# A gated DeltaNet layer: one decay matrix per unit in place of two

## The chip, the cores and the metric

One core of one Trainium2 chip runs the whole program in one launch. The metric is device time in microseconds. Three timed runs gave 2041.48, 2045.49 and 2047.63 us, so the median is 2045.49 us.

## What is computed

A trunk of two layers over 1024 tokens of width 1024, all in float32. The first layer is a gated DeltaNet, the second a softmax attention with a forget gate; the change lies in the first alone. Its core, for one value head and one chunk of tokens, with `g` the running sum of the log decay inside the chunk:

```python
decay = exp(where(lower, g[:, None] - g[None, :], -inf))
L = where(strict, (k * beta) @ k.T * decay, 0.0)
T = triangular_solve(eye + L, eye)
u = T @ (v * beta);  w = T @ (k * beta * exp(g))
attn = (q @ k.T) * decay
v_new = u - w @ state
o = (q * exp(g)) @ state + attn @ v_new
state = state * exp(g[-1]) + (k * exp(g[-1] - g)).T @ v_new
```

`k` and `q` are normalised to length one per token. There are 8 key heads and 16 value heads, so two value heads share the keys and queries of one key head. The output is normalised per head, multiplied with a gate `silu(z)` and projected back to width 1024.

## The kernel before

The tokens are taken in two halves of 512, each half in four chunks of 128 (the kernel's chunk; the result doesn't depend on it). A **unit** is one key head with its two value heads for one half: 8 groups x 2 halves = 16 units. For each unit the projections write keys, queries and values with the channels on the partitions, and then these stages run:

- `prepk`: `decay(t, "d1")` makes the matrix `d1[p, f] = exp(g_p - g_f)` for p > f, zero elsewhere, for 2 heads x 4 chunks (8 blocks of 128x128). It loads the row of `g` to all partitions (`gb`, 512 KB), masks it on GpSimd (`affine_select`) and takes eight exponentials on ScalarE. Then the keys are transposed (`to_tokens`), the strengths `un`, `wn` and `weg` are made from `beta` and the key norms `rk`, and `L` is written over `d1` as `wn * (k k^T) * d1`.
- `invert_blocks`: the 16x16 blocks on the diagonal of I + L are inverted by substitution on VectorE (`xi`, `xtmp`), with DMAs through DRAM (`lb`, `lr`, `rb`) that bring them to a suitable layout and back into `r` (`rmat`).
- `invert_merge`: three doubling steps of small matmuls (16, 32 and 64 wide) fill `r`, which holds the inverse transposed. VectorE makes the transposed diagonal blocks `tm` (`tmat`) with `nc.vector.transpose` on lines 1095 and 1125 and a scaling on line 1150. In each step the first matmuls read `lm` and `r`, the second ones read `tm`.
- `prepv`: the queries and values are transposed; the values are scaled by `un` on GpSimd (line 921).
- `prep2`: `decay(t, "d2")` makes `d2[s, t] = exp(g_t - g_s)` for t >= s, with a second load of `gb`, a second mask and eight more exponentials; then `exp(gb)` scales the queries (`qd`) and `d2` becomes the attention matrix `am`.
- `chain`: four chunks one after the other. `ch` matmuls give `k^T state` and then `T` times the corrected values, both in PSUM tile `p1`; `vn` (ScalarE copy, line 973) and `ve` (VectorE, line 974) are taken from `p1`; the `co` matmuls use them for the output and the new state.
- `finish`: the output of a unit is normalised, transposed, gated (`ogt`), split into a high and a low part (`ogh`, `ogl`) and stored.

TensorE's instruction order is written out by a planner, `Flow`, at build time: every stage is a generator that yields estimated waits (constants named `Y_...`, in ns), and whoever is due goes next. The projections have the last priority and fill what is left. The other engines' order comes from a scheduler with a model of time. Every engine then runs its own list in order, and every DMA is issued by SyncE in order. `at(shape, name, bufs)` takes a tile from a ring of `bufs` buffers: `gb` has 1, `d1` and `d2` have 2 each.

A matrix is split into a high and a low part for the projections (`mm3`: three matmuls for each pair).

Of the kernel before, what the change touches and what calls it, by code (L numbers as in the profile page):

```python
# [8 lines left out]
F32 = mybir.dt.float32  # L9
F32R = mybir.dt.float32r  # L10
# [5 lines left out]
P = 128  # L16
D = 1024
# [20 lines left out]
Y_PK = 1200  # L38
# [4 lines left out]
Y_P2 = 4000  # L43
# [10 lines left out]
Y_F1 = 800  # L54
Y_F2 = 2550
# [127 lines left out]
def tile_trunk(  # L183
# [308 lines left out]
    with ExitStack() as sa:  # L492
# [34 lines left out]
        def start_norm():  # L527
            xsT = [at([P, HALF], n, b) for n, b in (("k", KQ), ("k", KQ), ("k", KQ), ("q", 2), ("q", 2))]
            xsT += [at([P, HALF], "ktok", 3) for _ in range(3)]
            for t in range(CPH):  # L530
                xt = at([P, D], *(("vtok", 3), ("qd", 2))[t // 2])
                nc.sync.dma_start(xt, x[t * P : (t + 1) * P, :])
                for d in norm_tile(xt, at([P, D], "ogt", 1), lambda k, p, t=t: nc.scalar.copy(
                    xsT[k][:, t * P : (t + 1) * P], p)):
                    flow.t += d
            tags = [("d1", 2), ("og", 2), ("zg", ZG), ("d1", 2), ("og", 2), ("zg", ZG), ("gb", 1)]
# [10 lines left out]
            for n in range(2):  # L547
                ps = banks[n]
                acc = at([P, D], "d2", 2)
# [43 lines left out]
        def norm_tile(xt, jk, evac):  # L593
            rs = rms_rows(xt, jk, at)
# [13 lines left out]
        def next_norm():  # L608
            yield from hold(lambda: done["kqv"] >= 2)
            for t in range(CPH):  # L610
# [6 lines left out]
                hf = at([P, KT, P], "nh", 1)  # L617

                def evac(k, p):
                    nc.vector.tensor_scalar(  # L620
                        hf[:, k], p, gcol[0][:, k : k + 1], scol[0][:, k : k + 1],
                        op0=ALU.mult, op1=ALU.add,
                    )

                yield from norm_tile(xt, hf.rearrange("p k t -> p (k t)"), evac)
                yield 3000
                nc.sync.dma_start(
                    h1_d[:, :, t * P : (t + 1) * P].rearrange("k p t -> p k t"), hf
                )
# [12 lines left out]
        def gates(h, gt):  # L642
# [44 lines left out]
            nc.scalar.activation(ex, ex, AF.Exp)  # L687
            ngc = at([P, CPH, 16], "g_ngc", 2)
# [12 lines left out]
            gt.update(col=col, ex=ex, ngc=ngc, beta=beta, g_d=g_d)  # L701
# [132 lines left out]
        def decay(t, name):  # L834
            gb = at([P, 2, HALF], "gb", 1)
# [5 lines left out]
            dv = at([P, 2 * CPH, P], name, 2)  # L841
            low = name == "d1"
            nc.gpsimd.affine_select(
                out=dv, in_=gb.rearrange("p j (c t) -> p (j c) t", t=P),
                compare_op=ALU.is_gt if low else ALU.is_ge, fill=BIG if low else -BIG, base=0,
                pattern=[[0, 2 * CPH], [-1 if low else 1, P]], channel_multiplier=1 if low else -1,
            )
            bias = t["gt"]["col" if low else "ngc"]
            yield Y_DG
            for j in range(2):  # L850
                for c in range(CPH):
# [4 lines left out]
                        dv[:, u], dv[:, u], AF.Exp, scale=-1.0 if low else 1.0, bias=bias[:, c, hd : hd + 1]  # L856
                    )
            return gb, dv

        def prepk(t):  # L860
            g, gt, kf = t["g"], t["gt"], t["k"]
            _, d1v = yield from decay(t, "d1")
            yield Y_PK
            t["ktok"] = ktok = at([P, CPH, P], "ktok", 3)
            t["ss"] = ss = at([P, 2, CPH], "gss", 3)
# [3 lines left out]
            nc.vector.tensor_scalar(rk, ss[:, 0], EPS, None, op0=ALU.add)  # L869
            nc.gpsimd.tensor_tensor(rk, rk, mhalf[:, 0:CPH], op=ALU.pow)  # L870
            rkb = bc(rk, 2, 2)
            t["un"] = un = at([P, CPH, 2], "un", 3)
            t["wn"] = wn = at([P, CPH, 2], "wn", 2)
            t["weg"] = weg = at([P, CPH, 2], "weg", 3)
            nc.vector.tensor_tensor(un, gt["beta"][:, :, 2 * g : 2 * g + 2], rkb, op=ALU.mult)
            nc.vector.tensor_tensor(wn, un, rkb, op=ALU.mult)
            nc.vector.scalar_tensor_tensor(
                weg, wn, -1.0, gt["ex"][:, 1, :, 2 * g : 2 * g + 2], op0=ALU.mult, op1=ALU.mult
            )
            t["lm"] = d1v  # L880
# [27 lines left out]
        def prepv(t):  # L908
# [4 lines left out]
            for j in range(2):  # L913
                yield Y_PT
                yield from to_tokens(vt[:, j], vtok[:, :, j], None)
# [4 lines left out]
            for c in range(CPH):  # L920
                nc.gpsimd.tensor_tensor(vtok[:, c], vtok[:, c], bc(t["un"][:, c], 2, P), op=ALU.mult)
            yield 0

        def prep2(t):
            kf, qf = t["k"], t["q"]
            gb, d2 = yield from decay(t, "d2")
            t["am"] = am = d2.rearrange("p (j c) t -> p j c t", c=CPH)
            t["qd"] = qd = at([P, 2, CPH, P], "qd", 2)
            for j in range(2):
                yield 2 * Y_DX  # L930
                nc.scalar.activation(gb[:, j], gb[:, j], AF.Exp)
# [12 lines left out]
        def chain(t):  # L944
            h, g, gt, kf, r = t["h"], t["g"], t["gt"], t["k"], t["r"]
            ktok, qd, am, uv, weg, epo, ex = t["ktok"], t["qd"], t["am"], t["uv"], t["weg"], t["epo"], gt["ex"]
# [3 lines left out]
            for c in range(CPH):  # L950
# [4 lines left out]
                else:  # L955
                    mm(p1[:, 0:256], kf[:, c], st)
                    xt = at([P, 2 * P], "xp", 2)
                    for j in range(2):
                        sl = slice(j * P, (j + 1) * P)
                        nc.vector.scalar_tensor_tensor(  # L960
                            xt[:, sl], p1[:, sl], weg[:, c, j : j + 1], uv[:, c, j],
# [4 lines left out]
                for j in range(2):  # L966
# [6 lines left out]
                nc.scalar.copy(vn, p1[:, 256:512])  # L973
                nc.vector.tensor_tensor(
                    ve, p1[:, 256:512].rearrange("p (j f) -> p j f", f=P),
                    bc(ex[:, 0, c, 2 * g : 2 * g + 2], 2, P), op=ALU.mult,
# [36 lines left out]
        def finish(t, og, so):  # L1013
# [10 lines left out]
            ogt = at([P, 2, HALF], "ogt", 1)  # L1024
            for j in range(2):
                tr = yield from pst("tr", 2)
                for c in range(CPH):
                    tr_(tr[:, c * P : (c + 1) * P], og[:, c, j], ident)
                nc.vector.scalar_tensor_tensor(
                    ogt[:, j], tr, nw_h, zg[:, j], op0=ALU.mult, op1=ALU.mult  # L1030
                )
                flow.free(tr, R_T)
                yield Y_F1 if j == 0 else Y_F2
            ogh = at([P, 2, HALF], "ogh", 1, F32R)
            ogl = at([P, 2, HALF], "ogl", 1, F32R)
            for j in range(2):
                split(ogh[:, j], ogl[:, j], ogt[:, j], lo_eng=nc.vector)
                yield 1500
# [783 lines left out]
```

## Time and profile before

| | |
|---|---|
| median of three runs | 2045.49 us |
| the profiled execution's own time | 2046.11 us |
| its span, first to last instruction | 2044.3 us |
| TensorE busy (matmul) | 1852.2 us, 91% |
| VectorE busy | 1378.0 us, 67% |
| ScalarE busy | 1036.5 us, 51% |
| GpSimd busy | 484.5 us, 24% |
| mean granted TensorE clock | 0.954 of 2.4 GHz |

The profile is of one execution. "Busy" is the time in which at least one instruction of an engine runs; matmul ends are modelled. A wait names the instruction whose semaphore came last. PE is the matmul part of TensorE, PEld its weight loads, DVE VectorE, ACT ScalarE, POOL GpSimd and SP SyncE, which issues the DMAs. `d` stands for both decay matrices in the rows, `g_gc` marks the exponentials of the first and `g_ngc` those of the second. The units of the DeltaNet layer run from about 85 us to about 1100 us of the span; the output projection of that layer and the second layer follow.

### The profile page before, as it was taken

The numbers are of one execution on the slowest core, as the hardware profiler recorded it, in microseconds if no ns is written. First come the engines' busy times: TensorE is split into PE (matmuls) and PEld (weight loads), VectorE is DVE, ScalarE is ACT, GpSimd is POOL, SyncE is SP. The second block draws the span as 40 slices with busy tenths as digits, with TensorE's granted clock in tenths as the row PEclk, the third lists the DMA queues.
The fourth block names the chain that finished last, engine by engine and source line by source line (L and its number), as shares of the span: only waits on it lengthen the run. The fifth ranks groups of instructions, "written<-read, shape, count | busy, mean of one in ns | idle before, by whom it ended". The sixth has DMA issues, their size and how long they took to land.

```text
span 2044.3 us, 36353 instructions
## 1 busy us (share of the span) xinstructions
PE 1852.2 (91%) x12940; PEld 1546.6 (76%) x12940; DVE 1378.0 (67%) x3319; ACT 1036.5 (51%) x2684; POOL 484.5 (24%) x518
## 2 busy tenths in 40 slices
PE   4888898898998989999989788999999999999898
PEld 4666677777776777777877677889889889889676
DVE  5788888787868566766656576446656666666664
ACT  3554566555545445555444444246655655655631
POOL 2050232121213021222101322421231331331222
PEclk7988899999999999999999989999999999999899
DMA  6677676666555445454469988210210220111523
GB/s 246 222 244 236 199 254 198 217 228 219 184 175 158 153 142 175 155 154 131 143 216 316 306 307 279 80 53 32 63 60 19 60 65 21 58 62 38 170 84 96
DMA packets 236870, 317.83 MB, mean 155 GB/s; under 512 B 103752, under 2 KB 156512, under 8 KB 236688
## 3 DMA queue, kind: packets, MB, share of 16 engines
q1 hardware_dynamic: 236688, 315.51, 47.6%
q8 instruction: 102, 1.67, 0.3%
q14 instruction: 80, 0.66, 0.1%
HBM read 233.76 MB, written 81.67 MB: 154 GB/s over the span
## 4 chain that ended last, share of the span: by engine, by line
PE 54%; DVE 16%; DMA 16%; ACT 5%; issue 4%; SPq 3%; POOL 2%; DVEq 0%; POOLq 0%; ACTq 0%
PE mm L128 35%; PE lg L128 5%; PE pt L132 3%; PE oT L128 3%; DVE wlo L327 2%; PE tr L132 2%; PE co L128 2%; PE su L128 2%; DMA lr<-lb 2%; DMA wraw<-in_wb_dram 2%; DMA oraw<-in_ada_w_dram 2%; DVE cv_y L746 2%; DVE xtmp L1068 1%; DVE d L887 1%; DVE xi L1072 1%
## 5 line engine op out<-in xcount | busy, mean ns | idle before, releaser
L128 PE MATMUL mm<-ht_h,whi 128*128 128x512 f32 x784 | 352.8, 450 | 11.0 <-DVE olo L300 8.0
L128 PE MATMUL mm<-ht_l,whi 128*128 128x512 f32 x784 | 318.2, 406 | 3.9 <-DVE ht_l L583 3.9
L128 PE MATMUL mm<-ht_h,wlo 128*128 128x512 f32 x784 | 318.3, 406 | 1.7 <-POOL wlo L327 1.7
L128 PE MATMUL mm<-whi,h_h 128*128 128x384 f32 x512 | 186.9, 365 | 1.4 <-ACT whi L324 1.4
L128 PEld LDWEIGHTS mm<-ht_h,whi 128*128 128x128 f32 x784 | 154.9, 198 | 43.7 <-DVE olo L300 9.0
L128 PEld LDWEIGHTS mm<-ht_h,wlo 128*128 128x128 f32 x784 | 153.9, 196 | 37.7 <-POOL wlo L327 2.2
L128 PEld LDWEIGHTS mm<-ht_l,whi 128*128 128x128 f32 x784 | 155.2, 198 | 30.8 <-DVE ht_l L583 5.2
L128 PE MATMUL mm<-wlo,h_h 128*128 128x384 f32 x512 | 174.1, 340 | 2.7 <-POOL wlo L327 2.7
L746 DVE SCALAR_TENSOR_TENSOR cv_y<-cv_t,conv_h,cv_y 128x512 f32<-128x512 f32 x192 | 146.1, 761 | 42.3 <-ACT cv_y L738 40.1
L128 PE MATMUL mm<-whi,h_l 128*128 128x384 f32 x512 | 173.4, 339 | 0.0
L1562 DVE TENSOR_TENSOR ptl<-pt,pth 128x512 fp32r<-128x512 f32 x192 | 106.3, 555 | 85.2 <-ACT pth L1561 83.4
L1561 ACT CAST pth<-pt 128x512 fp32r<-128x512 f32 x192 | 91.2, 476 | 131.1 <-PE pt L132 130.1
L1405 POOL TENSOR_TENSOR rs<-ss,mhalf 128x4 f32<-128x4 f32 x64 | 64.5, 1007 | 314.4 <-DVE ss L1403 309.0
L327 DVE TENSOR_TENSOR wlo<-ht_h,whi 128x512 fp32r<-128x512 f32 x124 | 94.1, 802 | 52.9 <-ACT whi L324 46.5
L1526 ACT ACTIVATE lg<-lg,mx 128x896 f32<-128x896 f32 (+7 forms) x128 | 99.5, 778 | 54.5 <-DVE mx L1518 50.3
L324 ACT CAST whi<-ht_h 128x512 fp32r<-128x512 f32 x124 | 70.6, 619 | 103.7 <-DMA ht_h<-in_wa_o_dram 34.1
L128 PEld LDWEIGHTS mm<-wlo,h_h 128*128 128x128 f32 x512 | 97.7, 191 | 6.4 <-POOL wlo L327 4.4
L128 PEld LDWEIGHTS mm<-whi,h_h 128*128 128x128 f32 x512 | 98.2, 192 | 4.0 <-ACT whi L324 1.7
L128 PE MATMUL mm<-h_h,whi 128*128 128x512 f32 x240 | 100.5, 419 | 0.6 <-DVE wlo L1661 0.3
L324 ACT CAST whi<-wlo 128x512 fp32r<-128x512 f32 (+1 forms) x108 | 62.6, 626 | 72.8 <-PE mm L128 34.4
L132 PE MATMUL pt<-ident,lg 128*128 128x128 f32 (+1 forms) x584 | 96.0, 274 | 3.0 <-ACT lg L1526 3.0
L128 PEld LDWEIGHTS mm<-whi,h_l 128*128 128x128 f32 x512 | 97.1, 190 | 0.0
(355 smaller groups left out, 4715.6 us busy)
## 6 DMA issues: line engine op xcount, KB each, us to landing
ht_h<-in_wa_o_dram SPq DMA_DIRECT2D x62, 512.0 KB
wc<-whi SPq DMA_DIRECT2D x45, 512.0 KB
wc<-wlo SPq DMA_DIRECT2D x45, 512.0 KB
wlo<-wc SPq DMA_DIRECT2D x45, 512.0 KB
whi<-wc SPq DMA_DIRECT2D x45, 512.0 KB
wlo<-in_wa_c_dram SPq DMA_DIRECT2D x35, 512.0 KB
oraw<-in_ada_w_dram SPq DMA_DIRECT2D x128, 128.0 KB
gb<-g_d SPq DMA_DIRECT2D x32, 512.0 KB
```

What stands on the lines that cost most here:

```text
L128: self.nc.tensor.matmul(out, lhsT, rhs, start=start, stop=stop)
L132: self.nc.tensor.transpose(out, src, ident)
L324: nc.scalar.copy(hi, src)
L327: (lo_eng or nc.gpsimd).tensor_tensor(lo, src, hi.bitcast(F32), op=ALU.subtract)
L746: nc.vector.scalar_tensor_tensor(y, raw[:, j : j + HALF], w[:, j : j + 1], y, op0=ALU.mult, op1=ALU.add)
L887: nc.vector.scalar_tensor_tensor(d1v[:, u], mq[:, c * P : (c + 1) * P], wn[:, c, j : j + 1], d1v[:, u], op0=ALU.mult, op1=ALU.mult,)
L1068: nc.vector.tensor_tensor(tv, bc(lr[:, j + 1 :, j], 1, m), xi[:, 0:m, j : j + 1].broadcast_to([P, m, n]), op=ALU.mult,)
L1072: nc.vector.tensor_tensor(xi[:, 0:m, j + 1 :], xi[:, 0:m, j + 1 :], tv, op=ALU.subtract)
L1405: nc.gpsimd.tensor_tensor(rs, ss, mhalf[:, 0:4], op=ALU.pow)
L1526: nc.scalar.activation(lg, lg, AF.Exp, scale=-1.0, bias=mx[:, hh : hh + 1], accum_out=sums[:, tt : tt + 1],)
L1561: nc.scalar.copy(ph_[:, cs], pp[:, cs])
L1562: nc.vector.tensor_tensor(pl_[:, cs], pp[:, cs], ph_[:, cs].bitcast(F32), op=ALU.subtract)
```

## The change

- One decay matrix per unit. `decay` makes only `d2` (mask, eight exponentials) and takes `exp(gb)` right behind. `prepk` calls it ahead of the transposes of the keys; `prep2` makes none.
- `lm` is now a tile of its own (ring `d1`), written as `wn * (k k^T) * d2`, so it is the transpose of what it was, with the strength `wn` on the other side (a similarity by a diagonal). The inverse then acts on values that carry no strength: `xp` is `uv - exp(g) * (k^T state)` (`neg`), the values are divided by the key norm where they are taken from PSUM (ScalarE with `scale=irk`, four operations of 128x256 in place of two copies of 128x512 and four products on GpSimd), and `wn` is applied behind the inverse: `vn` is two scaled ScalarE operations of 128x128 in place of one copy of 128x256, and `ve` is scaled by `wex`.
- In `invert_merge` the roles swap: the first matmuls of each step read `lm` and `tm`, the second ones read `r`.
- Rings: `gb` 2 (was 1), `d2` 3 (was 2). The tiles `ogt`, `ogh`, `ogl` and `nh` hold half of what they did, one buffer each: `finish` now does one head at a time (transpose, gate, split, store with two DMAs of 256 KB), and the normalisation of the second half of the tokens stores in two pieces.
- Planner constants: `Y_PK` 1200 to 1000, `Y_P2` 4000 to 3000, `Y_F1` 800 to 900, `Y_F2` 2550 to 1600.

```diff
 def decay(t):
-    gb = at([P, 2, HALF], "gb", 1)
+    gb = at([P, 2, HALF], "gb", 2)
...
-    dv = at([P, 2 * CPH, P], name, 2)
+    dv = at([P, 2 * CPH, P], "d2", 3)
...
+    for j in range(2):
+        yield 2 * Y_DX
+        nc.scalar.activation(gb[:, j], gb[:, j], AF.Exp)
     return gb, dv
 def prepk(t):
-    _, d1v = yield from decay(t, "d1")
-    yield Y_PK
+    t["gb"], t["d2"] = yield from decay(t)
     yield from to_tokens(kf, ktok, ss[:, 0])
...
+    t["lm"] = lm = at([P, 2 * CPH, P], "d1", 2)
     nc.vector.scalar_tensor_tensor(
-        d1v[:, u], mq[:, c * P : (c + 1) * P], wn[:, c, j : j + 1], d1v[:, u],
+        lm[:, u], mq[:, c * P : (c + 1) * P], wn[:, c, j : j + 1], t["d2"][:, u],
 def prepv(t):
+    nc.scalar.activation(
+        vtok[:, c].rearrange("p j f -> p (j f)"), tr[:, o : o + 2 * P], AF.Copy,
+        scale=t["irk"][:, c : c + 1],
+    )
...
-    for c in range(CPH):
-        nc.gpsimd.tensor_tensor(vtok[:, c], vtok[:, c], bc(t["un"][:, c], 2, P), op=ALU.mult)
 def chain(t):
-    nc.scalar.copy(vn, p1[:, 256:512])
+    for j in range(2):
+        nc.scalar.activation(
+            vn[:, j * P : (j + 1) * P], p1[:, 256 + j * P : 256 + (j + 1) * P], AF.Copy,
+            scale=wn[:, c, j : j + 1],
+        )
 def finish(t, og, so):
-    ogt = at([P, 2, HALF], "ogt", 1)
     for j in range(2):
...
+        ogt = at([P, HALF], "ogt", 1)
...
+        ogh, ogl = at([P, HALF], "ogh", 1, F32R), at([P, HALF], "ogl", 1, F32R)
+        split(ogh, ogl, ogt, lo_eng=nc.vector)
 def invert_merge(t):
-    mm(pbk[b][o : o + 16, us], lm[sls[b], u, o : o + 16], r[sls[b], u, o + 16 : o + 32])
+    mm(pbk[b][sls[b], us], lm[h16, u, sls[b]], tms[b][0:16, u, 0:16])
...
-    mm(pa_[0:32, us], lm[32:64, u, 0:32], r[32:64, u, 32:64])
+    mm(pa_[32:64, us], lm[0:32, u, 32:64], tm[0:32, u, 0:32])
...
-    mm(p2[0:64, u * 64 : u * 64 + 64], lm[64:128, u, 0:64], r[64:128, u, 64:128])
+    mm(p2[64:128, u * 64 : u * 64 + 64], lm[0:64, u, 64:128], tm[0:64, u])
```

## Rows read from the trace of the kernel before

**Rows 1.** Windows by stage: busy us per engine, granted clock, DMA share, GB/s.

```profile
core 0: us, PE busy (x) PEld busy (x) DVE busy (x) ACT busy (x) POOL busy (x), PEclk, DMA share, GB/s
85.00:1100.00 1015.00, 909.05 (x7907) 738.33 (x7907) 752.46 (x1899) 532.86 (x1592) 218.24 (x274) 0.95 0.61 194
1100.00:1300.00 200.00, 174.30 (x746) 139.99 (x745) 123.03 (x204) 78.53 (x155) 54.97 (x42) 0.92 0.83 282
1300.00:2045.00 745.00, 713.93 (x4061) 622.19 (x4059) 451.07 (x1129) 388.38 (x854) 196.06 (x169) 0.98 0.19 62
```

**Rows 2.** Waits of PE from 85 to 1100 us: total, times, longest.

```profile
PE co L128 <- DVE ve L974: 19.2, 15, 2.4
PE tr L132 <- ACT vtok L905: 16.6, 6, 7.0
PE ch L128 <- DVE xp L960: 12.1, 9, 2.6
PE su L128 <- DMA rmat<-rb: 9.3, 2, 7.7
...
PE co L128 <- ACT vn L973: 7.9, 8, 2.9
PE tr L132 <- ACT ktok L905: 6.4, 1, 6.4
```

**Rows 3.** Groups by line and form, 85 to 1100 us: busy, mean ns, idle before.

```profile
L273 DVE SCALAR_TENSOR_TENSOR ohi<-oraw,cond,ohi 128x256 f32<-128x256 f32 x112 | 64.2, 573 | 14.2 <-DMA oraw<-in_ada_w_dram 13.6
...
L921 POOL TENSOR_TENSOR vtok<-vtok,un 128x256 f32<-128x256 f32 x64 | 44.6, 726 | 81.2 <-ACT vtok L905 81.2
...
L738 ACT ACTIVATE cv_y<-mm,conv_h 128x512 f32<-128x512 f32 x61 | 42.3, 694 | 0.0
...
L855 ACT ACTIVATE d<-d,g_ngc 128x128 f32<-128x128 f32 x128 | 40.9, 390 | 21.8 <-POOL d L843 21.8
L855 ACT ACTIVATE d<-d,g_gc 128x128 f32<-128x128 f32 x128 | 39.1, 390 | 24.1 <-POOL d L843 14.7 <-POOL cv_t L741 9.4
...
L843 POOL TENSOR_SCALAR_AFFINE_SELECT d<-gb 128x1024 f32<-128x1024 f32 x32 | 36.4, 1139 | 117.5 <-PE co L128 52.5 <-DMA gb<-g_d 39.0 <-PE su L128 17.1
...
L737 ACT COPY cv_t<-mm 128x512 f32<-128x512 f32 x60 | 35.1, 584 | 27.6 <-PE mm L128 27.4
...
L973 ACT COPY vn<-ch 128x256 f32<-128x256 f32 x63 | 23.6, 374 | 36.1 <-PE ch L128 35.9
...
L931 ACT ACTIVATE gb<-gb 128x512 f32<-128x512 f32 x32 | 18.4, 617 | 0.0
```

**Rows 4.** Timeline of ACT around the longest wait for `vtok`.

```profile
629.98 0.98 ACT L855 ACTIVATE d<-d,g_ngc 128x128 f32<-128x128 f32 x3 [1.77 <-POOL d L843]
...
632.20 1.26 ACT L855 ACTIVATE d<-d,g_ngc 128x128 f32<-128x128 f32 x4
633.37 0.56 ACT L905 COPY vtok<-tr 128x512 f32<-128x512 f32 x1
```

**Rows 5.** The window right behind that wait.

```profile
632.00:638.80 6.80, 4.82 (x14) 3.94 (x15) 3.42 (x6) 5.25 (x20) 4.11 (x4) 0.50 0.44 107
```

**Rows 6.** One line of VectorE in the whole trace: min/median/max ns.

```profile
L273 DVE SCALAR_TENSOR_TENSOR ohi<-oraw,cond,ohi x112: 430/480/1555, 91.9 to 617.7; 128x256 f32<-128x256 f32 x112
L746 DVE SCALAR_TENSOR_TENSOR cv_y<-cv_t,conv_h,cv_y x192: 697/748/1476, 62.9 to 1011.0; 128x512 f32<-128x512 f32 x192
```

**Rows 7.** Waits of DVE from 85 to 1100 us.

```profile
DVE ve L974 <- ACT vn L973: 10.1, 11, 3.0
```

**Rows 8.** Timeline, first and last of twelve merge steps with late transposes.

```profile
157.60 0.39 PE L128 MATMUL su<-rmat,d 32*16 32x16 f32 x4 [7.66 <-DMA rmat<-rb]
...
160.39 0.44 DVE L1095 STREAM_TRANSPOSE tmat<-rmat 32x256 f32<-32x256 f32 x1
...
1051.98 1.32 DVE L1125 STREAM_TRANSPOSE tmat<-rmat 32x256 f32<-32x256 f32 x3
...
1052.02 0.24 PE L128 MATMUL su<-rmat,d 32*32 32x32 f32 x2 [0.45 <-ACT rmat L1120]
```

**Rows 9.** The chain that ended last: start, us, what; a 512 KB load.

```profile
951.67 6.03 DMA gb<-g_d
```

More of the change, by code (lines that the diff above doesn't have):

```diff
@@ L53 @@
 Y_F0 = 9000
-Y_F1 = 800
-Y_F2 = 2550
+Y_F1 = 900
+Y_F2 = 1600
 Y_R2 = 6400
@@ L593, in norm_tile @@
         def norm_tile(xt, jk, evac):
-            rs = rms_rows(xt, jk, at)
+            if jk is None:
+                ss = at([P, 2], "ln_s2", 2)
+                for c in range(2):
+                    nc.scalar.activation(
+                        at([P, HALF], "nh", 1), xt[:, c * HALF : c * HALF + HALF], AF.Square,
+                        accum_out=ss[:, c : c + 1],
+                    )
+                nc.vector.tensor_tensor(ss[:, 0:1], ss[:, 0:1], ss[:, 1:2], op=ALU.add)
+                nc.vector.tensor_scalar(ss[:, 0:1], ss[:, 0:1], 1.0 / D, EPS, op0=ALU.mult, op1=ALU.add)
+                rs = at([P, 1], "ln_rs", 2)
+                nc.gpsimd.tensor_tensor(rs, ss[:, 0:1], mhalf[:, 0:1], op=ALU.pow)
+            else:
+                rs = rms_rows(xt, jk, at)
             nc.vector.tensor_scalar(xt, xt, rs, None, op0=ALU.mult)
@@ L687, in gates @@
             nc.scalar.activation(ex, ex, AF.Exp)
+            neg = at([P, CPH, 16], "g_neg", 2)
+            nc.vector.tensor_scalar(neg, ex[:, 1], -1.0, None, op0=ALU.mult)
             ngc = at([P, CPH, 16], "g_ngc", 2)
@@ L700, in gates @@
             done["gates"] = h + 1
-            gt.update(col=col, ex=ex, ngc=ngc, beta=beta, g_d=g_d)
+            gt.update(neg=neg, ex=ex, ngc=ngc, beta=beta, g_d=g_d)
         def z_after(i):
@@ L912, in prepv @@
             vtok = at([P, CPH, 2, P], "vtok", 3)
-            for j in range(2):
+            for c0 in range(0, CPH, 2):
                 yield Y_PT
-                yield from to_tokens(vt[:, j], vtok[:, :, j], None)
+                tr = yield from pst("tr", 2)
+                for c in (c0, c0 + 1):
+                    for j in range(2):
+                        o = (2 * (c - c0) + j) * P
+                        tr_(tr[:, o : o + P], vt[:, j, c], ident)
+                for c in (c0, c0 + 1):
+                    o = 2 * (c - c0) * P
+                    nc.scalar.activation(
+                        vtok[:, c].rearrange("p j f -> p (j f)"), tr[:, o : o + 2 * P], AF.Copy,
+                        scale=t["irk"][:, c : c + 1],
+                    )
+                flow.free(tr, R_T)
             done["tr"] += 1
@@ L925, in prep2 @@
             kf, qf = t["k"], t["q"]
-            gb, d2 = yield from decay(t, "d2")
+            gb, d2 = t["gb"], t["d2"]
             t["am"] = am = d2.rearrange("p (j c) t -> p j c t", c=CPH)
@@ L945, in chain @@
             h, g, gt, kf, r = t["h"], t["g"], t["gt"], t["k"], t["r"]
-            ktok, qd, am, uv, weg, epo, ex = t["ktok"], t["qd"], t["am"], t["uv"], t["weg"], t["epo"], gt["ex"]
+            ktok, qd, am, uv, epo, ex = t["ktok"], t["qd"], t["am"], t["uv"], t["epo"], gt["ex"]
+            wn, wex, neg = t["wn"], t["wex"], gt["neg"]
             st = state[g]
@@ L972, in chain @@
                 ve = at([P, 2, P], "ve", 2)
-                nc.scalar.copy(vn, p1[:, 256:512])
+                for j in range(2):
+                    nc.scalar.activation(
+                        vn[:, j * P : (j + 1) * P], p1[:, 256 + j * P : 256 + (j + 1) * P], AF.Copy,
+                        scale=wn[:, c, j : j + 1],
+                    )
                 nc.vector.tensor_tensor(
                     ve, p1[:, 256:512].rearrange("p (j f) -> p j f", f=P),
-                    bc(ex[:, 0, c, 2 * g : 2 * g + 2], 2, P), op=ALU.mult,
+                    bc(wex[:, c], 2, P), op=ALU.mult,
                 )
```

119 lines of the change are left out of this document (55 added, 64 removed).

## The prediction

> **What bounds the kernel now.** I read the windows by stage first. The units run in a stretch of 1015 us; TensorE is busy for 909 of them at a mean granted clock of 0.95, so 106 us are idle, and the clock gives away some more. Neither ScalarE (533) nor GpSimd (218) is near full; VectorE, with 752, is second [rows 1]. The two stretches behind hold nothing that the diff touches. The matmuls and transposes are as many as before, so the time can only change through TensorE's waits and the clock behind them. The waits of TensorE in that stretch come second: they are scattered over the chain (`co` behind `ve` and `vn`, `ch` behind `xp`), over transposes that find their PSUM bank not yet emptied by ScalarE (`vtok`, `ktok`), and over the first unit's inverse (`rmat`) [rows 2]. No single wait is over 20 us in total, so no edit here is worth more than about 1%. Third, the groups by line give the prices [rows 3], and fourth the timeline shows how such a wait comes about: ScalarE works off a set of eight exponentials and two of `gb`, having waited 1.77 us for the mask, from 629.98 to 633.46, and only then empties the bank with `vtok`; TensorE stood still for 7.0 us over it [rows 2, 4]. The clock follows: behind that wait TensorE was granted 0.50, that is 1.2 GHz, for 6.8 us, in which it was busy for 4.82 [rows 5].
>
> **The sum, from 2046.1 us**, the profiled execution's own time (1.8 us around its span, 0.6 us above the median of the runs).
>
> *The set of exponentials that goes.* Per unit one mask, one load and eight exponentials go. On ScalarE that is 128 x 390 ns, a busy time of 39.1 us, and the 21.8 us in which it stood idle before the second set, waiting for the mask, goes with that place [rows 3]. (The sets that stay carry the label of the second, in the place of the first.) What TensorE gets of this is the waits that such a set caused. The 7.0 us wait stood behind a set of `prep2`, the place that goes: 7.0, and the half clock behind it took 4.82 / 2 = 2.4. The rest of `vtok` and `ktok`, 16.6 - 7.0 + 6.4 = 16.0 us, lies behind sets of both places. The sets halve in number, but those that stay grow by the two exponentials of `gb`, 2 x 617 ns; so I take a quarter, 4, between 0 and 9.6 (all of `vtok`). Together 13.4.
>
> *VectorE beside GpSimd.* GpSimd loses 44.6 us of products (line 921) and 16 x 1139 ns = 18.2 us of masks, 62.8 of its 218 us, or 29% [rows 1, 3]. What VectorE gains is not written anywhere, but its operations stretch in places: the line `ohi` has a median of 480 ns, a mean of 573 and single ones of 1555, while `cv_y` has 748 and at most 1476 [rows 3, 6]. If all of VectorE lost what `ohi` loses, 93 of 573 ns, that is 122 us, and 29% of it is 35. If nothing of the stretching is GpSimd's, it is 0. I take 20 us, a little over the middle, as only the upper end is measured. The Trainium skill (SBUF — State Buffer, section "SBUF: two separate sides") says that a GpSimd operation and a VectorE operation with two SBUF inputs exclude each other for the whole instruction. By that rule the price would be GpSimd's removed 62.8 us times VectorE's busy share of 0.74, an estimate of 46 us; the maximum of 1555 ns for `ohi` fits an operation that waited one out.
>
> Of 20 us of VectorE I pass on 8 to TensorE: VectorE ended 31.3 us of its waits at `ve` and `xp` alone [rows 2], because its queue is long, but with 74% busy more than half of what is freed falls into its own idle time. Bounds 0 and 20.
>
> *Loads.* 16 loads of 512 KB go, each of them some 6 us from issue to landing [rows 9], in a stretch with a DMA share of 0.61 [rows 1]. The small transfers of the inverse wait less beside them: 2 of the 9.3 us at `rmat`, bounds 0 and 9.3. The 32 stores more of `finish` move the same bytes.
>
> *The chain's copy.* `vn` becomes two operations with a scale from memory. One of 128x256 took 374 ns; four exponentials of 128x128, also with an operand from memory, took 1.26 us, the last 0.39, so one behind the other costs 0.29 [rows 3, 4]: 0.29 + 0.39 - 0.37 = 0.31 us more in each of 63 chunks. Lower bound: nothing, where ScalarE and TensorE have slack; upper bound 63 x 0.31 = 19.5. VectorE stood waiting for `vn` 11 times and TensorE 8 times [rows 2, 7]; those overlap, so I take 13 chunks, 4 us. Here a rule speaks against the change. The Trainium skill (PSUM — Partial Sum Buffer, section "PSUM bank collisions raise a hardware error") has every two engines kept apart on a bank and quadrant, reads against reads too, so `ve` can't start until both copies are through; the trace agrees in that `ve` waits for `vn` though it reads none of it [rows 7]. Were that on the path in every chunk, the sum would be 15.5 us longer.
>
> *The values' scaling.* A 128x512 evacuation with a scale takes 694 ns against 584 for the plain one [rows 3], so 110 for the operand. Four of 374 + 110 against two of 584 are 0.77 us per unit, 12 us over all. They lie in what ScalarE is freed of (39.1 + 21.8); without that they would lengthen each `vtok` wait by under 0.8. Nothing.
>
> *The merge's transposes come earlier.* The first matmuls of a step now need `tm`, for which only the second ones waited, so TensorE stops where VectorE is late with lines 1095, 1125 or 1150. I set the end of these beside the start of the step's first matmul for all 48 steps: in twelve VectorE is later. The first is unit 0 (160.83 against 157.60, 3.23 us), the last unit 15 (1053.30 against 1052.02, 1.28 us) [rows 8]; over 1.2 us are 3.23, 1.73, 2.15, 1.49, 2.36, 1.28 and 2.89, and all twelve add to 17.4. Behind the stopped matmul all of TensorE's list stands. Lower bound 0 (these transposes had nobody waiting and may be moved up), upper 17.4 plus seven dips of the clock at 2.4 each, 34. I take 5: five of the twelve are in units 0 to 2, where VectorE is fullest and gains most.
>
> *Halved output tiles.* With one buffer, the cast of a unit's second head must wait until the first head's store has landed. A 512 KB transfer took 6 us, half as much perhaps 3 (an estimate from [rows 9]); the planner leaves 0.9 us and four transposes. So up to 2 us in 16 units, 32, if ScalarE's and VectorE's lists stand and TensorE behind them; 0 if something else is in the lists' front. I take 2.
>
> *Two exponentials more ahead of the keys.* 2 x 617 ns matter where TensorE already waits for `ktok`, at the start of each half: 2 us. The small new vectors (`irk`, `wex`, `neg`), the pieces of the norm and the rings `gb` and `d2` at the start cost and give nothing that 106 us of idle time wouldn't hide.
>
> Sum: 13.4 + 8 + 2 - 4 - 5 - 2 - 2 = 10.4 us, so 2035.7, say **2036 us**.
>
> **Rivals.**
> *It cancels.* The matmul count is the same, ScalarE is half idle and GpSimd never was the bound. If only half of what depends on slack arrives (4 + 8 + 2 halved), it is 2043; if none, 2050. For it: 0.3% or 6 us is about what three runs can tell from no change, and my sum is barely over it. Against: the 7.0 us wait has its cause plainly in the set that goes.
> *TensorE waits for VectorE's transposes* (slower). One mechanism, at the first matmuls of the three merge steps. Price 34 instead of 5: 2036 + 29 = 2065; with the waits alone, 2036 + 12 + half of the dips, about 2056. It decides once the lateness costs 5 + 15.6 us (to 2051.6), that is 1.3 us per unit. For it: it is late in twelve of 48 steps now. Against: VectorE has less to wait for.
> *The stores of `finish`* hold ScalarE and VectorE: 2 us in 16 units, a good half passed on: 2036 + 18 = 2054.
> *VectorE's backlog breaks.* If three quarters of the waits for `ve` and `xp` go (23.5 instead of 8), it is 2020. For it: VectorE ends most of the chain's waits. Against: one of the two, `ve`, now stands behind a longer `vn`. By the skill's rule of the SBUF port, with 46 us freed and the same share passed on, it would be 2025.
>
> **The numbers.** Forecast (2028 to 2039) 0.38; backlog breaks 0.12; cancels, the copy on the path in every chunk included (2051), 0.26; transposes 0.17; stores 0.07. Faster by over 0.3% than 2045.49 is below 2039.4: 0.50; within: 0.26; slower: 0.24. The forecast's own range is 2028 to 2039; from 2018 to 2058 no more than 2 in 10 is left out.
>
> **What would show it.** The page after: GpSimd near 420 us busy, ScalarE near 1030, `ohi` with a mean near its median, sixteen `gb` loads. Right: waits of TensorE on `vtok` under 8 us, on `ve` and `xp` under 28. Wrong in the transposes: rows "su behind DVE tmat" in the waits of TensorE with over 10 us. Wrong in the copy: `co` behind `vn` over 15. Wrong in the stores: ScalarE's `ogh` behind a DMA. Since the planner's order shifts with the constants, stalls can also move to places that no row here names; a change of under 6 us would prove none of these.

## The result: 0.37% slower, and the profile after

The changed kernel takes 2050.07 us (median of 20 runs, 2043.35 to 2061.69) against 2044.39 (20 runs, 2038.28 to 2049.70): a ratio of 1.0037, 95% interval 1.0025 to 1.0050 (the medians alone give 1.0028, the means 1.0036). The forecast of 2036 had the direction wrong. The profiled execution took 2049.11 us with a span of 2047.2, so the two profiles differ by 3.0 us; the other 3 to 5 us lie in the scatter of the runs and no row shows them.

Windows of the changed kernel (columns as in [rows 1]): the units' stretch, the two behind it, then the units' stretch cut in two, into the start of the first half and the rest:

```profile
core 0: us, PE busy (x) PEld busy (x) DVE busy (x) ACT busy (x) POOL busy (x), PEclk, DMA share, GB/s
85.00:1100.00 1015.00, 908.35 (x7892) 739.47 (x7892) 728.29 (x1918) 523.67 (x1565) 147.09 (x194) 0.95 0.59 186
1100.00:1300.00 200.00, 171.76 (x741) 135.92 (x740) 126.42 (x204) 79.42 (x154) 52.68 (x36) 0.94 0.83 277
1300.00:2045.00 745.00, 717.60 (x4081) 625.06 (x4079) 454.31 (x1131) 389.97 (x857) 199.40 (x175) 0.99 0.20 63
85.00:215.00 130.00, 94.02 (x844) 74.44 (x844) 102.32 (x272) 63.17 (x176) 17.48 (x31) 0.86 0.72 234
215.00:1100.00 885.00, 814.33 (x7050) 665.03 (x7049) 625.97 (x1647) 460.50 (x1390) 129.61 (x163) 0.96 0.57 179
```

The start and the rest in the kernel before:

```profile
85.00:215.00 130.00, 103.80 (x886) 80.59 (x886) 109.82 (x282) 68.70 (x192) 34.14 (x42) 0.87 0.80 257
215.00:1100.00 885.00, 805.26 (x7022) 657.74 (x7022) 642.65 (x1617) 464.15 (x1400) 184.10 (x232) 0.96 0.59 185
```

The reliefs are all there: against [rows 1] GpSimd lost 71 us in the units' stretch, VectorE 24, ScalarE 9 (over the whole execution 71, 18 and 7). TensorE as a whole got nothing: 106.65 us idle instead of 105.95. But that is the sum of two changes. The start has 36.0 us instead of 26.2, and the rest of the units' stretch 70.7 instead of 79.7: 9.0 us were gained there, and 9.8 lost at the start.

The waits of TensorE, 85 to 1100 us, changed kernel:

```profile
PE co L128 <- DVE ve L1004: 18.4, 17, 5.2
PE su L128 <- DVE ln_s L601: 15.5, 1, 15.5
PE tr L132 <- ACT ktok L923: 11.6, 1, 11.6
PE tr L132 <- DVE vt L770: 7.6, 3, 4.2
PE tr L132 <- ACT vtok L940: 4.8, 2, 4.1
PE ch L128 <- DVE xp L986: 4.6, 4, 2.4
PE su L128 <- DVE tmat L1149: 4.3, 6, 1.2
...
PE co L128 <- ACT vn L1000: 2.4, 5, 0.7
...
PE tr L128 <- DVE tmat L1120: 1.5, 4, 0.7
PE mm L128 <- DVE olo L300: 1.4, 1, 1.4
```

(The row with `ln_s` is the wait of the first merge: the transpose that it needs ended at 169.52 us, and `ln_s`, a step of the norm that VectorE did next, at 169.57.)

Read by releaser, beside [rows 2], this looks like the forecast: `vtok` fell from 16.6 to 4.8, `xp` from 12.1 to 4.6, `vn` from 7.9 to 2.4. Read by the instruction that waits, the total did not move. The transposes of the values, before and after (groups by line: busy, mean ns, idle before them and what ended it):

```profile
L132 PE MATMUL tr<-ident,vt 128*128 128x128 f32 x128 | 22.3, 303 | 24.7 <-ACT vtok L905 16.1 <-ACT ktok L905 6.4 <-ACT sqt L901 1.5
```

```profile
L132 PE MATMUL tr<-ident,vt 128*128 128x128 f32 x128 | 22.4, 302 | 24.5 <-ACT ktok L923 11.6 <-DVE vt L770 7.6 <-ACT vtok L940 4.8
```

24.7 us became 24.5, but this sum hides the same two changes. The same group before, in the start and in the rest:

```profile
L132 PE MATMUL tr<-ident,vt 128*128 128x128 f32 x16 | 3.4, 353 | 7.1 <-ACT ktok L905 6.4 <-ACT vtok L905 0.7
L132 PE MATMUL tr<-ident,vt 128*128 128x128 f32 x112 | 18.9, 295 | 17.6 <-ACT vtok L905 15.4 <-ACT sqt L901 1.5 <-DVE ogt L1029 0.7
```

and after:

```profile
L132 PE MATMUL tr<-ident,vt 128*128 128x128 f32 x16 | 4.5, 422 | 16.2 <-ACT ktok L923 11.6 <-DVE vt L770 4.2 <-ACT sqt L919 0.4
L132 PE MATMUL tr<-ident,vt 128*128 128x128 f32 x112 | 18.0, 285 | 8.2 <-ACT vtok L940 4.8 <-DVE vt L770 3.4
```

In the rest of the stretch 9.4 us went: the waits for `vtok` of 2.30, 7.04, 2.24 and 3.80 us at 229, 634, 905 and 962 us, the one of [rows 4] among them, have no successor at the same unit. At the start 9.1 us came: the first unit's wait for `ktok` grew from 6.4 to 11.6, and the second unit's transposes wait 4.2 for `vt`.

Summed by the instruction that waits over TensorE's rows from 85 to 1100 us, the chain's products (`ch`, `co`) went from 40.7 to 33.0 us idle, the projections (`mm`) from 15.3 to 8.5, and the merge's products (tiles `rmat`, `tmat`, `pp`, `pq`, `qq`) from 17.5 to 31.0. So 14.5 us were gained, and 13.5 lost again in the merge, 8.3 of them at the start.

How the first merge comes late (timelines around the first unit's keys). ScalarE, changed kernel:

```profile
97.80 0.27 ACT L919 ACTIVATE sqt<-tr 128x128 bf16<-128x128 f32 x1
...
100.53 0.98 ACT L870 ACTIVATE d<-d,g_ngc 128x128 f32<-128x128 f32 x3 [2.37 <-POOL d L859]
101.42 1.13 ACT L875 ACTIVATE gb<-gb 128x512 f32<-128x512 f32 x2
102.46 1.55 ACT L870 ACTIVATE d<-d,g_ngc 128x128 f32<-128x128 f32 x5
...
104.17 0.97 ACT L870 ACTIVATE d<-d,g_ngc 128x128 f32<-128x128 f32 x3
105.05 1.13 ACT L875 ACTIVATE gb<-gb 128x512 f32<-128x512 f32 x2
106.09 1.55 ACT L870 ACTIVATE d<-d,g_ngc 128x128 f32<-128x128 f32 x5
...
108.71 0.58 ACT L923 COPY ktok<-tr 128x512 f32<-128x512 f32 x1
```

GpSimd and VectorE, changed kernel:

```profile
108.96 2.68 POOL L957 TENSOR_TENSOR qd<-q,gb 128x512 f32<-128x512 f32 x2 [3.70 <-DVE q L770]
111.60 1.06 POOL L888 TENSOR_TENSOR rk<-irk,mhalf 128x4 f32<-128x4 f32 x1
```

```profile
108.84 0.17 DVE L887 TENSOR_SCALAR irk<-gss 128x4 f32<-128x4 f32 x1
...
114.89 0.16 DVE L889 TENSOR_TENSOR irk<-irk,rk 128x4 f32<-128x4 f32 x1
...
169.10 0.42 DVE L1120 STREAM_TRANSPOSE tmat<-rmat 32x256 f32<-32x256 f32 x1
```

and VectorE of the kernel before at the same steps:

```profile
102.77 0.16 DVE L869 TENSOR_SCALAR rk<-gss 128x4 f32<-128x4 f32 x1
...
104.37 0.16 DVE L875 TENSOR_TENSOR un<-g_beta,rk 128x8 f32<-128x8 f32 x1
```

With two buffers `gb`, both the first and the second unit's sets, ten exponentials each, stand between the first and the third of the four squares of the keys: the squares are ready for VectorE at 108.84 instead of 102.77. Then GpSimd's power for `rk` stands behind two products `qd`, which can now be made early, and what follows `rk` on VectorE starts at 114.89 instead of 104.37. The last step of this unit's elimination (`xi`) starts at 157.54 instead of 146.05, its block loads `rmat` are issued at 165.8 instead of 152.7, and the merge starts at 169.58 instead of 157.60 [rows 8].

### The profile page after: what moved, and what is told of

Its sections match the earlier page's. It is cut to its first block, busy times and chain, and to the rows that moved or that the text cites. A ratio compares the mean times of both kernels' runs of the same rounds, so it can differ in the third digit from the quotient of the medians.

```text
span 2047.2 us, 36319 instructions
## 1 busy us (share of the span) xinstructions
PE 1852.6 (90%) x12940; PEld 1546.3 (76%) x12940; DVE 1360.1 (66%) x3341; ACT 1029.7 (50%) x2660; POOL 413.0 (20%) x438
## 4 chain that ended last, share of the span: by engine, by line
PE 60%; DVE 13%; DMA 12%; ACT 5%; issue 5%; SPq 2%; POOL 2%; DVEq 0%; POOLq 0%; ACTq 0%
PE mm L128 39%; PE lg L128 5%; PE su L128 3%; PE oT L128 3%; PE pt L132 3%; PE tr L132 3%; PE co L128 2%; DVE wlo L327 2%; DVE cv_y L763 2%; DMA wraw<-in_wb_dram 2%; PE ch L128 2%; DMA oraw<-in_ada_w_dram 1%; ACT whi L324 1%; POOL wlo L327 1%; DMA ohi<-og_d 1%
## 5 line engine op out<-in xcount | busy, mean ns | idle before, releaser
L128 PEld LDWEIGHTS mm<-ht_h,wlo 128*128 128x128 f32 x784 | 152.6, 195 | 37.5 <-POOL wlo L327 2.3
L763 DVE SCALAR_TENSOR_TENSOR cv_y<-cv_t,conv_h,cv_y 128x512 f32<-128x512 f32 x192 | 150.5, 784 | 33.4 <-ACT cv_y L755 30.6
L327 DVE TENSOR_TENSOR wlo<-ht_h,whi 128x512 fp32r<-128x512 f32 x124 | 98.3, 835 | 57.4 <-ACT whi L324 50.1
L324 ACT CAST whi<-ht_h 128x512 fp32r<-128x512 f32 x124 | 70.7, 618 | 94.4 <-PE mm L128 47.4
```

The lines of the kernel that those rows point to most:

```text
L128: self.nc.tensor.matmul(out, lhsT, rhs, start=start, stop=stop)
L324: nc.scalar.copy(hi, src)
L327: (lo_eng or nc.gpsimd).tensor_tensor(lo, src, hi.bitcast(F32), op=ALU.subtract)
L763: nc.vector.scalar_tensor_tensor(y, raw[:, j : j + HALF], w[:, j : j + 1], y, op0=ALU.mult, op1=ALU.add)
```

## The experiments

Ratios are to the kernel before in runs on the same chip, with 95% intervals (they can differ by 0.1% from the ratio of the medians); the last column is TensorE's idle time from 85 to 215 us in that run's profile (26.2 before, 36.0 changed). "TensorE's order" is the order of its instructions in the built program.

| run | built on | median us | ratio (interval) | idle at the start |
|---|---|---|---|---|
| e1 | changed | 2046.17 | 1.0017 (1.0001 to 1.0033) | 37.4 |
| e2 | changed | 2040.67 | 0.9984 (0.9967 to 1.0002) | 37.5 |
| e3 | changed | 2040.86 | 0.9999 (0.9981 to 1.0016) | 32.5 |
| e4 | before | 2049.23 | 1.0037 (1.0023 to 1.0051) | 25.1 |
| e7 | changed | 2051.76 | 1.0048 (1.0032 to 1.0065) | 34.4 |
| e10 | changed | 2057.55 | 1.0089 (1.0065 to 1.0113) | 35.0 |
| e6 | before | 2029.17 | 0.9937 (0.9916 to 0.9959) | 26.9 |
| e5 | before | 2039.10 | 0.9985 (0.9969 to 1.0001) | 25.1 |
| e15 | changed | 2057.47 | 1.0054 (1.0035 to 1.0073) | 33.5 |
| e16 | before | 2049.25 | 1.0032 (1.0018 to 1.0046) | 26.2 |
| e13 | changed | 2050.60 | 1.0024 (1.0006 to 1.0042) | 32.3 |
| c1 | changed | 2069.20 | 1.0115 (1.0093 to 1.0136) | 32.6 |
| c2 | changed | 2067.30 | 1.0110 (1.0090 to 1.0130) | 36.2 |
| c3 | before | 2053.69 | 1.0041 (1.0025 to 1.0057) | 24.3 |
| p1 | changed | 2050.37 | 1.0028 (1.0017 to 1.0039) | 34.1 |
| p3 | before | 2045.96 | 1.0002 (0.9985 to 1.0020) | 26.0 |
| e17 | before | 2061.50 | 1.0072 (1.0051 to 1.0092) | 26.5 |
| e8 | changed | 2046.85 | 0.9999 (0.9983 to 1.0015) | 33.9 |

### The start: one `gb` (e1), keys first (e2), the norm in one piece (e15)

```diff
-            gb = at([P, 2, HALF], "gb", 2)
+            gb = at([P, 2, HALF], "gb", 1)
...
                 yield from hold(lambda: "g_d" in ts[i]["gt"])
+                yield from hold(lambda: i == 0 or "qd" in ts[i - 1])
```

> The changed kernel, but with one buffer gb instead of two, so that the second unit of a half starts its decay matrix only when the first unit's products qd have read gb. Theory A (two whole sets of exponentials, 10 instructions each, stand ahead of the first unit's keys at the start of a half, and everything of that unit comes late): TensorE's wait for ktok between 85 and 1100 us falls from 11.6 us to 6 or 7, its wait at the first merge from 15.5 us to 8 or 9, and the time from 2050 us to 2038 to 2043. Rival B (the merge's transposes and output order cost it): within 3 us of 2050, and the waits for tmat (6.7 us in all) as before. Rival C (any other order of the units' steps moves the sum by several us either way): the two waits at the start fall, but the time does not follow them.

The ratio fell by 0.2%, about 4 us, with intervals that overlap. The second set left its place and the merge started at 156.97 us, but the wait for `ktok` stayed at 9.9 us, and the start is as idle as before the edit. TensorE stopped again inside the merge. TensorE and VectorE of that run:

```profile
156.97 0.28 PE L128 MATMUL su<-tmat,d 16*32 16x16 f32 x2 [8.24 <-DVE tmat L1121]
...
166.78 0.23 PE L128 MATMUL tr<-tmat,d 16*32 16x16 f32 x1 [8.60 <-DVE nh L634]
```

```profile
150.33 1.04 DVE L634 TENSOR_SCALAR nh<-tr,gcol,scol 128x128 f32<-128x128 f32 x3
...
165.36 1.37 DVE L634 TENSOR_SCALAR nh<-tr,gcol,scol 128x128 f32<-128x128 f32 x4
```

The fourth product of the merge needs a PSUM bank that still holds the norm's second four columns; `nh` has one half buffer, whose first store was issued only at 159.60, and VectorE emptied that bank at 166.7.

For e2 the plan issues the keys ahead of the exponentials:

```diff
-            yield Y_DG
+            yield Y_DG + 2 * CPH * Y_DX + 4 * Y_DX
+            yield from keys()
             for j in range(2):
                 for c in range(CPH):
-                    yield Y_DX
...
-            t["gb"], t["d2"] = yield from decay(t)
-            yield from to_tokens(kf, ktok, ss[:, 0])
+            t["gb"], t["d2"] = yield from decay(t, lambda: to_tokens(kf, ktok, ss[:, 0]))
```

> The changed kernel, but in prepk the key's squares and its transposes into ktok are issued ahead of the unit's ten exponentials (the same planned time in all). Theory A: no wait for ktok over 3 us is left between 85 and 1100 us, the first merge starts at about 158 us instead of 169.6, and the time is 2037 to 2043 us. Rival B (transposes of the merge): 2047 to 2053 us. Rival C (order): the waits at the start fall and the time stays, because equal stalls open later.

The time came as theory A said, and for another reason: the wait for `ktok` stayed at 11.6 us and the first merge's at 15.6, since the scheduler of the other engines put the exponentials in front again. What e2 changed is TensorE's order.

e15 is e1 with the norm of the kernel before:

```diff
-                    hf[:] = [at([P, 4, P], "nh", 1)]
...
+                hf = at([P, KT, P], "nh", 1)
...
-                yield from norm_tile(xt, None, evac)
+                yield from norm_tile(xt, hf.rearrange("p k t -> p (k t)"), evac)
```

> The changed kernel with one buffer gb (as in the first run) and with the second half's norm as in the kernel before (one whole buffer nh and one store for each token tile, not two halves that share a buffer, where the second half waits for the store of the first); TensorE's order stays that of the changed kernel. Theory E (the loss is made at the start, between 85 and 215 us, by waits in line: a second set of exponentials and gb's own ahead of ktok, GpSimd's power behind the products qd, and the norm's half buffer, which holds a PSUM bank of the merge): TensorE's idle time from 100 to 200 us falls from 35 or 36 us to 24 to 28, and the time to a ratio of 0.996 to 0.999 to the kernel before. Rival (one gb alone did all that can be had there): 1.001 to 1.003.

The stop at `nh` went, the start fell to 33.5 us only, and the time rose by 0.37% against e1. TensorE now waited 17.4 us for the merge's transposes, 8.8 of it at the second unit's first merge (190.88 us), whose block loads were issued only at 188.59: here too the load was late, and the transpose behind it. Theory E, as a list of three waits to be taken away, falls.

### The merge: more planned time (e3, e8), products without transposes (e13)

```diff
+            yield 2500
             yield from flow.both(("su", "tr"))
...
-Y_MR = 3000
+Y_MR = 4500
...
-Y_M1 = 2000
+Y_M1 = 3000
```

> The changed kernel with more planned time in the merge: 2500 ns before the first step that reads tmat, 4500 instead of 3000 and 3000 instead of 2000 ns before the next two, so that other units' work is issued between a transpose on VectorE and the product that reads it. Theory A: the waits for tmat (6.7 us in all) shrink, the time stays within 3 us of 2050. Rival B: the waits for tmat go below 2 us and the time falls by 5 to 7 us, to 2043 to 2045. Rival C (order): any value from 2040 to 2056 without a tie to these waits.

8 us better than the changed kernel and equal to the one before, a time near rival B's; but the waits for `tmat` fell from 6.7 us to 4.3 only, not below 2, and e3 also shifts TensorE's order. So e13 takes the transposes out with TensorE's order kept:

```diff
-lm[h16, u, sls[b]], tms[b][0:16, u, 0:16]
+lm[h16, u, sls[b]], r[h16, u, h16]
```

and so for the other two steps.

> The changed kernel, but the merge's products read rmat itself instead of its transposes tmat (values of the inverse change: a part of the computation is replaced), so that none of them waits for VectorE's transposes, which still run. Rival B (the transposes cost it): the time falls by 6 us or more, to a ratio of 1.001 or less. Theory E: the first merge still waits 13 us or more, now for rmat's load itself, and the ratio stays at 1.002 to 1.004.

The first merge now waits for the load itself (waits of TensorE, 85 to 215 us, that run: total, times, longest):

```profile
PE su L128 <- DMA rmat<-rb: 12.6, 1, 12.6
```

The ratio is 0.13% lower than the changed kernel's, less than the intervals' width. The merge is late because its unit is late; its transposes cost at most a few us. e8 puts e2's and e3's edits together:

> The changed kernel with both the keys issued ahead of the exponentials in the plan and more planned time in the merge. If the gains of the two single runs (11 and 8 us) are mechanisms that add up: a ratio of 0.993 to 0.996, faster than both kernels. If they were orders that happened to fall well: anywhere from 0.998 to 1.010.

The two gains of 11 and 8 us did not add up; together they give 0.38%. They are orders that fell well, not two mechanisms, and no version here beats the kernel before by more than can be measured.

### The chain's copy: alone (e4), taken out (e7), replaced (e10)

```diff
-                nc.scalar.copy(vn, p1[:, 256:512])
+                for j in range(2):
+                    nc.scalar.activation(vn[:, j * P : (j + 1) * P], ..., AF.Copy, scale=ones[:, c : c + 1])
```

> The kernel before with one part of the change alone: vn is copied out of PSUM by two instructions of ScalarE with a column as scale (a column of ones, so the values stay) instead of one plain copy. If the copy sits in every chunk's path: 63 times 0.31 us, so plus 15 to 20 us. If only chunks with ScalarE late pay (the forecast's term): plus 4 us. Theory A: 0 to 2 us, since TensorE's wait co<-vn fell from 7.9 to 2.4 us in the changed kernel although the copies are there.

Plus 0.37%, 7.5 us, with TensorE's order unchanged. The wait stands where the forecast put it, one step further: not at `vn` but at `ve`, 28.2 us instead of 19.2 [rows 2] (waits of TensorE, 85 to 1100 us, that run):

```profile
PE co L128 <- DVE ve L978: 28.2, 22, 2.6
```

Worked out from the records of 63 chunks, the two copies take 0.63 us from the first's start to the second's end instead of 0.37, and `ve` ends 2.66 us behind the last `ch` product instead of 2.37. So 0.26 us more of ScalarE's read delayed the end of VectorE's by 0.29. The rule of the Trainium skill that two engines are kept apart on a bank and quadrant (PSUM — Partial Sum Buffer, section "PSUM bank collisions raise a hardware error") agrees with that.

e7 gives the changed kernel the plain copy:

> The changed kernel with vn as one plain copy again, so that the strength is left out of the outputs inside a chunk (a part of the computation is left out); the order on TensorE stays. Theory D (the two scaled copies are the term that decides: alone in the kernel before they cost 0.37%): the time falls by 6 to 9 us, to a ratio of 0.999 to 1.001 to the kernel before, and TensorE's wait for ve falls. Rival (the forecast's size, 4 us or less, since the wait for vn is smaller in the changed kernel): a ratio of 1.002 to 1.004.

Theory D falls: nothing came back. In the changed kernel `ve` ends 2.29 us behind `ch` even with the long copies (62 chunks), and 2.12 without; VectorE starts it 0.67 us behind the long copies, where it took 0.94 in the kernel before. The copy's price is real in the kernel before; what covers it in the changed one is not shown. e10 keeps the computation and puts the strength on `am`:

```diff
-                nc.vector.tensor_tensor(am[:, j], mq.rearrange("p (c t) -> p c t", t=P), am[:, j], op=ALU.mult)
+                for c in range(CPH):
+                    nc.vector.scalar_tensor_tensor(am[:, j, c], mq[:, c * P : (c + 1) * P], t["wn"][:, c, j : j + 1], am[:, j, c], ...)
```

> The changed kernel with the same computation, but the strength as a factor on the rows of am (prep2 makes am by eight instructions of 128 x 128 with a column per unit instead of two of 128 x 512, some 0.9 us more of VectorE in each of 16 units) and vn as one plain copy. Theory D: as the run with the plain copy, less at most 16 x 0.9 us = 14 us of VectorE that is mostly hidden: a ratio of 0.999 to 1.002. Rival: 1.002 to 1.005, when VectorE's 14 us weigh as much as ScalarE's 19.

0.5% slower than the changed kernel, and 0.4% slower than e7, which has the same plain copies: VectorE's 6.6 us more (1366.7 against 1360.1 us busy over the whole execution) cost time, and ScalarE's saved copies gave none back.

### Other parts alone in the kernel before: e6, e5, e16, e17

e6 leaves out the loop of line 921.

> The kernel before without GpSimd's 64 products that scale the values (that part of the computation is left out); the order on TensorE stays. It shows what the relief of GpSimd and of VectorE beside it is worth alone. The forecast gave it 8 us (20 us of VectorE freed, 0.4 passed on), which makes a ratio of 0.996. Rival (VectorE's freed time is slack): 0.999 to 1.001. Rival (its whole backlog breaks): 0.990.

12.7 us faster, TensorE's order unchanged: the relief of GpSimd and VectorE is worth more than the 8 us of the forecast. The line from which it was argued, `ohi`, did not shorten (573 ns before, [rows 3]; its group in that run):

```profile
L273 DVE SCALAR_TENSOR_TENSOR ohi<-oraw,cond,ohi 128x256 f32<-128x256 f32 x112 | 63.7, 569 | 20.9 <-DMA oraw<-in_ada_w_dram 20.3
```

Other lines did. VectorE's busy time over the whole execution fell by 17.1 us (1378.0 to 1360.9), near the 20 of the forecast, and most of it lies in the small steps of the inverse: the 480 operations of `xtmp` and `xi` take 106.5 us in sum instead of 119.5 (median 0.19 us). In the kernel before, 52 of them take over 0.45 us, and each of these 52 ends within 0.06 us of the end of a GpSimd operation that runs beside it, in 31 cases one of line 921. In e6 18 such operations are left, in the changed kernel 5 (92.2 us in sum). One of them in the kernel before, and the mask beside it (ends at 123.49 and 123.45 us):

```profile
122.36 1.09 POOL L843 TENSOR_SCALAR_AFFINE_SELECT d<-gb 128x1024 f32<-128x1024 f32 x1 [3.74 <-DMA gb<-g_d]
122.40 1.09 DVE L1072 TENSOR_TENSOR xi<-xi,xtmp 128x30 f32<-128x30 f32 x1
```

The Trainium skill's rule of the shared port (SBUF — State Buffer, section "SBUF: two separate sides"), by which a GpSimd operation and a VectorE operation with two SBUF inputs exclude each other, agrees with these pairs; the price by it, an estimate of 44.6 x 0.74 = 33 us, is twice what e6 shows. TensorE's waits for `ve` and `xp` fell from 31.3 to 25.2 us, for `olo` from 8.0 to 4.7, for `vn` from 7.9 to 3.5; its idle time behind the start fell from 79.7 to 67.9.

e5 has `finish` by heads (the diff's lines of `finish`, with its two constants and the scratch tile `nx` in place of a borrowed `ogt`).

> The kernel before with finish by heads alone (half output tiles, split and stored one head after the other, with the planned times of the changed kernel). The forecast gave it plus 2 us with ends 0 and 32: a ratio of 1.001. If half tiles make ScalarE wait on the stores of the first head: 1.004 and more, and a wait of ScalarE for a DMA at ogh. It changes the order on TensorE too, so that an effect of up to 4 us either way may be order alone.

No loss, as far as a run that shifts TensorE's order can say. The feared wait exists, 6.3 us in this run and more in the changed kernel (waits of ScalarE, 85 to 1100 us), but it is ScalarE that stands there:

```profile
ACT ogh L324 <- DMA og_d<-ogh: 21.4, 7, 5.2
```

e16 has the diff's `norm_tile` and `next_norm`, e17 those and e4's copies.

> The kernel before with the norm in halves alone (two tiles of four column blocks that share one buffer, each stored by itself). Theory E: VectorE and ScalarE wait some 10 us for the stores of nh (10.2 us in the changed kernel), and TensorE for a part of it: a ratio of 1.001 to 1.004. Rival (the waits are hidden, the forecast's zero): 0.999 to 1.001.

> The kernel before with the two scaled copies of vn and the norm in halves together, TensorE's order as before. If the prices add up: 7.5 + 6.5 = 14 us, a ratio of 1.0055 to 1.008. If the second is paid out of the same waits as the first: 1.003 to 1.0045.

The norm in halves, which the forecast set at nothing, costs 0.32%, 6.5 us. Its own waits in the profile are small (TensorE 3.1 us for `nh`), so which stall carries the price is not shown. Both parts together cost 0.72%, against 0.37 + 0.32 = 0.69: in the kernel before the prices add up.

### Order alone: c1, c2, c3, p1, p3

```diff
-SC = 1.0
+SC = 1.01
```

(c2: 0.99; c3 on the kernel before; p1 and p3: `HP = 1300` instead of 1000)

> The changed kernel with every planned wait 1% longer and nothing else, so that the order of the same instructions shifts on all engines. It measures what order alone does. Theory C (order decides over several us): a ratio anywhere from 0.999 to 1.008. Theory E: 1.002 to 1.005, with 33 us or more of idle time from 100 to 200 us.

> The changed kernel with every planned wait 1% shorter and nothing else. Theory C (order decides, the change itself is worth less than the orders differ): a ratio anywhere from 0.996 to 1.010. Theory E (the change's own waits at the start cost, order is small): 1.002 to 1.006.

> The kernel before with every planned wait 1% longer and nothing else. Theory C: a ratio from 0.995 to 1.010, as far from 1 as the changed kernel's own 1.0037. Theory E: 0.998 to 1.002.

> The changed kernel with the lead of the preparing steps 1300 instead of 1000, which leaves TensorE's order as it is and moves some 5% of VectorE's instructions and 1% of ScalarE's and GpSimd's to other places. It measures how much the order on the other engines does when TensorE's stays. If it does as much as in the runs that kept TensorE's order (0 to 10 us), their differences can't be read one by one: a ratio of 0.999 to 1.008. If not: 1.003 to 1.005.

> The kernel before with the same lead of 1300 instead of 1000, TensorE's order as before. Theory C: a ratio of 0.996 to 1.005; otherwise within 0.1% of 1.

A shift of the planned waits by 1% made the changed kernel 0.78% and 0.73% slower still, and the kernel before 0.41% slower; the first two are more than either theory had allowed. Moving the other engines' instructions with TensorE's order kept did next to nothing (1.0028 against 1.0037, 1.0002 against 1). So, going by these two runs alone, runs that keep TensorE's order (e1, e4, e6, e7, e10, e13, e15, e16, e17) can be read to about 0.2%, and those that shift it (e2, e3, e5, e8) can't be read for their edit at all.

## Why the prediction was wrong

- **The start: the step that failed.** The prediction gave "two exponentials more ahead of the keys" 2 us, and let the pieces of the norm and the rings `gb` and `d2` at the start cost "nothing that 106 us of idle time wouldn't hide". TensorE's idle time is no room in which a cost disappears; it is the sum of the waits, and at the start it grew by 9.8 us. A whole second set stands ahead of the keys, and the power behind `qd`. The start is idle for 32.3 to 37.5 us in all twelve profiles of kernels with the change, and for 24.3 to 26.9 in all eight without: some 9 us, the one loss that no order removed, and as much as was gained behind the start. The single edits (e1, e15, e13) each uncovered the next wait, so which of them would have to go together stays open.
- **The pieces of the norm, nothing**: 6.5 us alone in the kernel before, so the same reason failed here too. In the changed kernel the price is not shown: e15, which takes the pieces out of e1, was slower than e1.
- **The set of exponentials that goes, 13.4 us** (11.0 of waits, 2.4 of the clock): the mechanism was right. Behind the start the transposes of the values wait 8.2 us instead of 17.6, which is 9.4 of the 11.0. In the seven profiles with the changed kernel's TensorE order they wait 8.2 to 11.0 us there, in the six with the order of the kernel before 16.5 to 21.4. Under other orders they wait 3.0 to 21.1, and no run took the set alone out of the kernel before, so a part of the 9.4 may be order. At the start the same transposes lost 9.1.
- **VectorE beside GpSimd, 8 us**: the mechanism was right (e6: VectorE freed of 17.1 us, where the text took 20) and its worth to TensorE mis-sized (e6: 12.7). It came through `xtmp` and `xi`, not through `ohi`.
- **The merge's transposes, 5 us**: rows "su behind DVE tmat" came to 5.2 us, under the 10 that the text named. The merge's products lost 13.5 us all the same, 8.3 of it at the start, behind a late `rmat`, where e13 leaves the transposes 2.9 of 15.5 us.
- **The chain's copy, 4 us**: 7.5 us alone in the kernel before, nothing to be had back in the changed one.
- **The stores of `finish`, 2 us**: the sign named for "wrong" came (ScalarE's `ogh` behind a DMA, 21.4 us); no cost shows, as far as e5 can tell, which shifts TensorE's order.

Nearly every sign of "right" that the prediction named came true (GpSimd 413.0 us busy, ScalarE 1029.7, sixteen `gb` loads, `vtok` 4.8, `ve` and `xp` 23.0 us), but for `ohi`, and the time went the other way. Of the rivals "it cancels" (2043 to 2050) was nearest in its number, by luck: it said that the gains would not arrive, and they arrived behind the start (9.0 us) and were lost at the start (9.8). That is shown for the two profiles; p1 and p3, the same two TensorE orders, have 6.7 gained and 8.1 lost. That the last 3 to 5 us are the change's own is not: three other orders of the same changed kernel (e2, e3, e8) are equal to the kernel before, two are 1.1% slower, and the kernel before loses 0.41% by the same kind of shift. Whether one decay matrix is slower in itself stays open; in the order given it is.

## What to carry to other kernels

Cut a sum of waits by stage before reading it: 24.7 and 24.5 us looked like no change and were a gain of 9.4 and a loss of 9.1. Idle time of the busiest engine is made of waits, so it hides no new cost that stands in front of one. Price a wait by the instruction that stands still, and list every input that it needs with its time: when the last one is made faster, the second last is the gain's limit (without the transposes, e13's first merge waited 12.6 us instead of 15.5). When a planner lays out an engine's order, time two or three arbitrary orders of the same kernel first; an effect smaller than their spread can be read only from runs that keep that order. A second buffer lets the next unit's work into the queues ahead of this unit's: check the queue at the start of a pipeline, where nothing else is there to fill. (Taking the buffer away again, in e1, moved the first merge but did not shorten the start.)

## What was not expected of the hardware

A power on GpSimd of only 128x4 values took 1.22 us on average (16 in the units' stretch), as long as the mask of 128x1024 (1.24 us), so the smallest step of the keys can be the one that a queue turns into a stop. And operations of GpSimd held up VectorE's until they ended: of the small steps `xtmp` and `xi`, with a median of 0.19 us, one took 1.09 beside a mask in the kernel before. The longest `ohi` of the changed kernel, 2564 ns (median 481), lies beside a GpSimd operation `wlo` of 2.67 us, and all eight over 600 ns have one of GpSimd's beside them.
